# Attention on one Trainium2 core: the closing steps of a group loaded earlier and spread over the ticks

## The chip, the cores and the metric

The kernel runs on one core of a Trainium2 chip. A core has TensorE (PE, matrix products into PSUM), VectorE (DVE), ScalarE (ACT), GpSimd (POOL), and SyncE (SP), which in this kernel issues all DMAs. Each engine takes its instructions strictly in order. The metric is the device time of one execution in microseconds (us).

## The reference

A decoder trunk of two layers over 2048 tokens of width 1024. Layer 0 runs a gated recurrence (RG-LRU) and multi-head latent attention side by side, gates both with SiLU and projects them back; layer 1 is a Mamba-2 scan. What matters here is the attention of layer 0 and its gate:

```python
for blk in range(seqlen // Q_BLOCK):
    s = (jnp.einsum('bqhd,bkhd->bhqk', q_nope[:, q0:kend], k_nope[:, :kend])
         + jnp.einsum('bqhr,bkr->bhqk', q_rope[:, q0:kend], k_rope[:, :kend]))
    s = jnp.where(mask, s * scale, -jnp.inf)
    p = jax.nn.softmax(s, axis=-1)
    outs.append(jnp.einsum('bhqk,bkhd->bqhd', p, v[:, :kend]))
...
y = jnp.concatenate([y_rnn, y_mla], axis=-1) * jax.nn.silu(gate)
return jnp.einsum('bse,ed->bsd', y, w_out)
```

There are 8 heads, 64 value channels each. All matrix products are made in split precision: an operand is a high part and a low part, and three products (high-high, high-low, low-high) are summed, or two where one operand is exact enough.

## The kernel before

The program runs layer 0's projections and recurrence, then the attention (some 460 to 1005 us in the profile), the output projection of layer 0, the scan of layer 1 and its output projection. Between 1005 us and the end PE has few gaps.

**Groups.** Attention works in 32 groups. A group is a triple (pr, c, e): a pair of heads pr, a chunk c of 512 queries, and the head e of the pair. `GROUPS` (L35) lists them; a pair takes 8 groups, c from 3 down to 0, each for both heads (the last pair in another order). A group with chunk c looks at c+1 chunks of keys, so c=3 is the longest and c=0 the shortest. The texts number the groups 0 to 31 in this order: group 8 is the first of the second pair.

**Ticks.** One loop (L836 to 847) writes the program. For each group it goes through its score banks: `bank` (L736 to 751) makes three products of 128 queries with up to 512 keys (L740 to 742, on the diagonal also a mask, L744), and DVE takes the row maximum (L745). After each bank `tick()` advances a counter, and functions put off by `later(lag, fn)` are then written out. `expo` (ACT, L761), the sums (L769, L772) and the write of 1/sum to DRAM (L774) are put off in this way. L774 writes 128 x 4 numbers to a row of `d_li`, four bytes at a time. Between the banks of group n the loop writes the transposes (`trans`, L785) of the probabilities of the group before, each followed by a tick, then ACT's cast (L791), DVE's low part (`lo`, L129) and, five transposes later, the product with V (`pv`, L812).

**The split of q.** Group n+1 needs its q as high and low part in a slot of `ring`. `split_q(n + 1)` (L705 and one `lo`, both on POOL) stands after the second bank of group n, the load of q for group n+2 (`load_q`, L701) after the third. The first product of a group (L740) needs the first part, the third (L742) the second.

**The closing steps of a group.** `pv` adds up y for 512 queries in one PSUM bank. Two key blocks before its end SP loads 1/sum back from DRAM, spread over the 64 partitions of the head (`li`, L808), and the gate `g` (L809). The tiles `li`, `g` and `y` exist once, one half of the partitions for each head. When the last product is written, follow: one tick later ACT's copy of half of the bank to y (L818) and POOL's g*li (L819), after two ticks DVE's addition of the other half (L822), after three POOL's y*g (L826), after five the store of y (L829) to `d_y`. So POOL's queue holds L819 and L826 of one group right before a split of q for a later group, and SP's queue holds each store before later loads.

**After the last group** the loop from L865 drains what is left, and among it reads the first four tiles of `d_y` for the output projection (`out0_load`, L894) and splits two (L900). In the last groups POOL also splits six weight matrices for that projection (L114, L129).

Of the kernel before, what the change touches and what calls it, by code (L numbers as in the profile page):

```python
# [31 lines left out]
NV0 = 35  # L32


GROUPS = [(pr, c, e) for pr in range(4) for c in ((3, 1, 0, 2) if pr == 3 else (3, 2, 1, 0)) for e in range(2)]  # L35


EL, TL, LAG, SLACK = 3, 1, 5, 4
# [19 lines left out]
class K:  # L58
# [96 lines left out]
    def run(self):  # L155
        nc, tc, A = self.nc, self.tc, self.A
        with ExitStack() as ctx:
# [20 lines left out]
            D["x1T"] = dp.tile([NCH, P, KB, 2, 512], F32R, name="d_x1T")  # L178
            D["li"] = dp.tile([len(GROUPS), 512], F32, name="d_li")
            D["cs"] = dp.tile([NT, 32, P], F32, name="d_cs")  # L180
# [460 lines left out]
    def phase_qkv(self):  # L641
# [28 lines left out]
        self.qst = {}  # L670
        for n, (pr, c, e) in enumerate(GROUPS):
            if n < 8:
# [25 lines left out]
    def load_q(self, n):  # L698
        pr, c, e = GROUPS[n]
        self.qst[n] = self.stp.tile([P, 512], F32, tag="st", name="st")  # L700
        self.nc.sync.dma_start(out=self.qst[n], in_=self.D["q"][2 * pr + e, c])  # L701
# [6 lines left out]
    def phase_attn(self):  # L708
        nc, A, p, v = self.nc, self.A, self.at, self.nc.vector
        vv = self.W[:, 0:8, :].rearrange("p h (k n) -> p h k n", n=128)  # L710
        ring, D = self.ring, self.D
        N = len(GROUPS)

# [7 lines left out]
        prp = self.prp()  # L721
        prob, sums, accs = {}, {}, {}
        ready, flow = [], []

        def scores(n, i):

            pr, c, e = GROUPS[n]
            q = ring[:, 8 + n % 2, :]
# [48 lines left out]
        def trans():  # L777

            n, kb = ready.pop(0)
            pr, c, e = GROUPS[n]  # L780
            i0 = max(0, kb - 4 * c)
            ps = self.psum()
            for i in range(i0, 4):
                o = 512 * c * i + 64 * i * (i + 1) + kb * 128
                nc.tensor.transpose(ps[:, i * 128:i * 128 + 128], prob[n][:, o:o + 128], self.ident)  # L785
            self.cnt += 1
            k = self.cnt % 6
            hl = self.W[:, 8 + k // 2, k % 2 * 1024:k % 2 * 1024 + 1024] if k < 4 else ptx[:, k - 4]
            hl = hl.rearrange("p (s n) -> p s n", s=2)
            w = slice(128 * i0, 512)  # L790
            self.later(TL, lambda: nc.scalar.copy(hl[:, 0, w], ps[:, w]))  # L791
            self.later(TL + 1, lambda: self.lo(v, hl[:, 1, w], ps[:, w], hl[:, 0, w]))
            flow.append((n, kb, hl, w))
            if kb == 4 * c + 3:
                prob[n] = None
            if len(flow) > LAG:
                pv()
            self.tick()

        def pv():  # L800

            n, kb, hl, w = flow.pop(0)
            pr, c, e = GROUPS[n]
            nkb = 4 * c + 4
            if kb == 0:
                accs[n] = self.psum()
            if kb == nkb - 2:
                nc.sync.dma_start(out=li[half(e)], in_=D["li"][n].partition_broadcast(64))  # L808
                nc.sync.dma_start(out=g[half(e)], in_=D["sg"][pr, half(e), c * 512:c * 512 + 512])  # L809
            acc = accs[n]  # L810
            for s in range(2):
                nc.tensor.matmul(acc[:, w], vv[:, 2 * pr + e, kb], hl[:, s, w],  # L812
                                 start=(kb == 0 and s == 0), stop=(kb == nkb - 1 and s == 1))
            if kb == nkb - 1:
                r, o = half(e), half(1 - e)

                def copy():
                    nc.scalar.copy(y[r], acc[o])  # L818
                    nc.gpsimd.tensor_tensor(out=g[r], in0=g[r], in1=li[r], op=ALU.mult)  # L819

                def add():
                    v.tensor_tensor(out=y[r], in0=y[r], in1=acc[r], op=ALU.add)  # L822
                    accs.pop(n)

                def fin():
                    nc.gpsimd.tensor_tensor(out=y[r], in0=y[r], in1=g[r], op=ALU.mult)  # L826

                def store():
                    nc.sync.dma_start(out=D["y0"][4 * c:4 * c + 4, r, 4 + pr, :].rearrange("t p n -> p t n"),  # L829
                                      in_=y[r].rearrange("p (t n) -> p t n", n=P))  # L830
                self.later(1, copy)
                self.later(2, add)
                self.later(3, fin)
                self.later(5, store)

        for n in range(N):  # L836
            pr, c, e = GROUPS[n]
# [12 lines left out]
            k = n - (N - 9)  # L850
            if 0 <= k < 6:
                self.load_at(0, k, A["wo0"][k], 7, (nc.gpsimd, nc.gpsimd))
        k, old, ws = 0, True, []
# [11 lines left out]
        while ready or flow or any(d[1].__qualname__.endswith("expo") for d in self.defer):  # L865
            while todo and todo[0][0] <= k:
                todo.pop(0)[1]()
            if old and k > 3 and not any(x[0] < N - 1 for x in ready + flow):
                old = False
                self.later(2, lambda: last_w(0))  # L870
            k += 1
            if ready:
                trans()
            else:
                if flow:
                    pv()
                self.tick()
# [714 lines left out]
```

## Time and profile before

| | |
|---|---|
| median of three runs | 2729.05 us (2728.33 to 2729.82) |
| the profiled execution | 2731.9 us, of which the span of the program is 2729.8 |
| busy in the span | PE 2629.1 us (96%), DVE 1746.3, ACT 1532.1, POOL 940.2 |
| attention, from the first scores to the last product | 462.7 to 1005.4 us |
| granted clock of PE, mean | 0.985 |

A busy PE is not a PE at its peak, since matmuls overlap in the records. A row's idle time stands in brackets behind it, with what ended it. The page cuts the span into 40 slices of 68 us, and the row PEclk tells the granted clock in tenths of full speed (9 is 90% or more).

### The profile page before, as it was taken

How to read it: one execution, taken by the hardware profiler on the slowest of the kernel's cores; microseconds unless marked ns; L12 is line 12 of the kernel's file. 1: busy time of each engine (PE TensorE's matmuls, PEld its weight loads, DVE VectorE, ACT ScalarE, POOL GpSimd, SP SyncE). 2: the span in 40 equal slices, each digit the busy share in tenths (PEclk: the TensorE clock that was granted, in tenths of full speed). 3: DMA queues.
4: the chain of work that ended last, by engine and by line, in shares of the span. 5: the costliest groups of instructions: out<-in, count | busy, mean ns of one | idle time of the engine just before them, and what ended most of it. 6: DMA issues, size and time to landing. Idle time of an engine off the chain costs nothing.

```text
span 2729.8 us, 40041 instructions
## 1 busy us (share of the span) xinstructions
PE 2629.1 (96%) x14504; PEld 2168.2 (79%) x14504; DVE 1746.3 (64%) x3245; ACT 1532.1 (56%) x3178; POOL 940.2 (34%) x880
## 2 busy tenths in 40 slices
PE   8999999989898899999999999999999999899998
PEld 6888977868787777878888888888888888778886
DVE  7776236868686656775667766676677666745532
ACT  5664345757676652224667766776667667642100
POOL 5455320132324435452234323442244232433421
PEclk9999999989898999999999999999999999999999
DMA  4133337131424235666234333443234324456421
GB/s 146 53 95 103 109 112 262 35 68 41 69 44 81 65 105 193 214 237 192 79 125 157 124 110 106 146 142 110 99 122 143 110 102 141 158 175 216 164 106 39
DMA packets 173110, 334.22 MB, mean 122 GB/s; under 512 B 31985, under 2 KB 90225, under 8 KB 169457
## 3 DMA queue, kind: packets, MB, share of 16 engines
q1 hardware_dynamic: 172912, 331.66, 38.5%
q8 instruction: 115, 1.88, 0.3%
q14 instruction: 83, 0.67, 0.1%
HBM read 245.82 MB, written 85.79 MB: 121 GB/s over the span
## 4 chain that ended last, share of the span: by engine, by line
PE 68%; DVE 11%; DMA 7%; ACT 7%; issue 3%; POOL 2%; SPq 1%; POOLq 0%; ACTq 0%; DVEq 0%
PE ps L1148 8%; PE ps L1150 8%; PE ps L1149 8%; PE ps L137 5%; PE ps L139 5%; PE ps L138 5%; DMA g<-d_sg 3%; PE ps L1397 3%; PE ps L1398 3%; PE ps L1396 3%; PE ps L785 3%; PE ps L812 3%; PE ps L1251 2%; PE ps L910 1%; PE ps L742 1%
## 5 line engine op out<-in xcount | busy, mean ns | idle before, releaser
L1148 PE MATMUL ps<-ring,W 128*128 128x512 f32 x768 | 304.7, 397 | 0.0
L1150 PE MATMUL ps<-ring,W 128*128 128x512 f32 x768 | 300.2, 391 | 0.0
L1149 PE MATMUL ps<-ring,W 128*128 128x512 f32 x768 | 299.2, 390 | 0.0
L745 DVE TENSOR_REDUCE mx<-ps 128x1 f32<-128x512 f32 (+3 forms) x320 | 192.9, 607 | 114.3 <-PE ps L744 58.0
L1270 POOL TENSOR_TENSOR y<-y,xs 128x512 f32<-128x512 f32 x60 | 78.7, 1311 | 427.3 <-DVE y L1269 427.3
L761 ACT ACTIVATE pr<-ps,mx 128x512 f32<-128x512 f32 (+3 forms) x320 | 198.5, 629 | 14.9 <-DVE mx L749 10.0
L1148 PE MATMUL ps<-W,ring 128*128 128x512 f32 x512 | 201.3, 393 | 0.0
L1150 PE MATMUL ps<-W,ring 128*128 128x512 f32 x512 | 200.4, 391 | 0.0
L1149 PE MATMUL ps<-W,ring 128*128 128x512 f32 x512 | 199.9, 390 | 0.0
L785 PE MATMUL ps<-cst,pr 128*128 128x128 f32 x1088 | 181.3, 282 | 7.5 <-ACT pr L761 5.4
L1201 ACT ACTIVATE e<-e,tab 128x128 f32<-128x128 f32 x512 | 156.4, 390 | 42.6 <-DMA e<-d_cs 42.6
L1150 PEld LDWEIGHTS ps<-ring,W 128*128 128x128 f32 x768 | 144.1, 188 | 31.0
L1148 PEld LDWEIGHTS ps<-ring,W 128*128 128x128 f32 x768 | 144.4, 188 | 29.8 <-ACT yo L1302 0.9
L1149 PEld LDWEIGHTS ps<-ring,W 128*128 128x128 f32 x768 | 144.4, 188 | 28.9
L791 ACT CAST W<-ps 128x512 fp32r<-128x512 f32 (+2 forms) x213 | 110.8, 524 | 100.5 <-PE ps L785 98.6
L785 PEld LDWEIGHTS ps<-cst,pr 128*128 128x128 f32 x1088 | 133.9, 145 | 41.7 <-ACT pr L761 9.4
L129 DVE TENSOR_TENSOR W<-ps,W 128x512 fp32r<-128x512 f32 (+3 forms) x261 | 144.4, 559 | 30.6 <-ACT W L613 18.8
L740 PE MATMUL ps<-ring 128*128 128x512 f32 (+3 forms) x320 | 122.9, 384 | 37.6 <-POOL ring L705 34.4
L1116 ACT ACT_TABLE_LOAD x58 | 74.4, 1283 | 148.6 <-DVE xT L1114 79.2
L1381 ACT CAST ring<-ring 128x1024 fp32r<-128x1024 f32 x50 | 50.4, 1045 | 188.7 <-PE ps L1397 100.5
L129 POOL TENSOR_TENSOR ring<-ring 128x1024 fp32r<-128x1024 f32 (+1 forms) x41 | 84.1, 2051 | 190.4 <-ACT ring L1381 180.2
L129 POOL TENSOR_TENSOR W<-st,W 128x512 fp32r<-128x512 f32 (+2 forms) x70 | 111.4, 1597 | 103.7 <-ACT W L112 86.3
(347 smaller groups left out, 7552.3 us busy)
## 6 DMA issues: line engine op xcount, KB each, us to landing
ring<-d_x1T SPq DMA_DIRECT2D x128, 512.0 KB, 7.7
e<-d_cs SPq DMA_DIRECT2D x64, 512.0 KB, 4.5
ring<-d_y SPq DMA_DIRECT2D x25, 1024.0 KB, 7.8
st<-in_w_dram SPq DMA_DIRECT2D x40, 512.0 KB, 4.6
d_x1T<-xt SPq DMA_DIRECT2D x32, 512.0 KB, 3.1
d_y<-yo SPq DMA_DIRECT2D x64, 256.0 KB, 5.5
st<-in_wo_dram SPq DMA_DIRECT2D x24, 512.0 KB, 4.7
xs<-in_xT_dram SPq DMA_DIRECT2D x23, 512.0 KB, 4.3
```

Of the source, the lines that this page charges most:

```text
L129: eng.tensor_tensor(out=out, in0=src, in1=hi.bitcast(F32), op=ALU.subtract)
L137: self.nc.tensor.matmul(ps, ah, bh, start=(i == 0), stop=False)
L138: self.nc.tensor.matmul(ps, ah, bl, start=False, stop=False)
L139: self.nc.tensor.matmul(ps, al, bh, start=False, stop=(i == n - 1))
L740: nc.tensor.matmul(ps[:, 0:nw], qh, k[:, 0:nw], start=True, stop=False)
L745: v.tensor_reduce(out=m[:, kc:kc + 1], in_=ps[:, 0:nw], axis=AX.X, op=ALU.max, negate=True)
L761: nc.scalar.activation(out=prob[n][:, o:o + nw], in_=ps[:, 0:nw], func=AF.Exp, bias=nm, accum_out=acc)
L785: nc.tensor.transpose(ps[:, i * 128:i * 128 + 128], prob[n][:, o:o + 128], self.ident)
L1148: nc.tensor.matmul(ps, ah, bh, start=(k == 0), stop=False)
L1149: nc.tensor.matmul(ps, ah, bl, start=False, stop=False)
L1150: nc.tensor.matmul(ps, al, bh, start=False, stop=(k == KB - 1))
L1201: nc.scalar.activation(out=e[:, hd], in_=e[:, hd], func=AF.Relu, scale=-1.0, bias=cs[:, hd:hd + 1])
```

## The change

It does two things. In `pv` and in the steps behind it, the loads of `li` and `g` are written eight key blocks before a group's end (at the fourth block where the group is shorter) instead of two, and g*li, y*g and the store are cut apart: g*li moves from one tick after the last product to four, y*g from three to six, the store from five to ten; for c=0 to 8, 10 and 14. Before the loads of a group whatever is left of the last group of the same head is written out (`end[e]`). The copy (ACT) and the addition (DVE) stay. And the last pair takes its chunks in the order 3, 0, 1, 2 instead of 3, 1, 0, 2.

```diff
-GROUPS = [(pr, c, e) for pr in range(4) for c in ((3, 1, 0, 2) if pr == 3 else (3, 2, 1, 0)) for e in range(2)]
+GROUPS = [(pr, c, e) for pr in range(4) for c in ((3, 0, 1, 2) if pr == 3 else (3, 2, 1, 0)) for e in range(2)]
...
+        end = [lambda: None, lambda: None]
...
-            if kb == nkb - 2:
+            if kb == max(3, nkb - 8):
+
+                end[e]()
                 nc.sync.dma_start(out=li[half(e)], in_=D["li"][n].partition_broadcast(64))
                 nc.sync.dma_start(out=g[half(e)], in_=D["sg"][pr, half(e), c * 512:c * 512 + 512])
...
                 def copy():
                     nc.scalar.copy(y[r], acc[o])
+
+                def gate():
                     nc.gpsimd.tensor_tensor(out=g[r], in0=g[r], in1=li[r], op=ALU.mult)
...
                 self.later(1, copy)
                 self.later(2, add)
-                self.later(3, fin)
-                self.later(5, store)
+                left = [gate, fin, store]
+
+                def upto(k):
+                    while len(left) > k:
+                        left.pop(0)()
+                end[e] = lambda: upto(0)
+                for at, k in ((4, 2), (6, 1), (10, 0)) if c else ((8, 2), (10, 1), (14, 0)):
+                    self.later(at, lambda k=k: upto(k))
```

On SP, at the end of the first pair: the store of group 2 (d_y), the k loads for the next pair (ring<-d_k), the writes of 1/sum of groups 4 and 5 (d_li<-ls), the q loads of groups 7 and 8 (st<-d_q), the loads li and g of groups 3 and 4, and the store of group 3. Before:

```order
L829 DMA d_y_72<-y 64x4x128
L687 DMA ring<-d_k 64x1024
L774 DMA d_li<-ls_3759 128x4x1
L701 DMA st<-d_q 128x512
L808 DMA li<-d_li 64x512
L809 DMA g<-d_sg 64x512
L687 DMA ring<-d_k 64x1024
L829 DMA d_y_72<-y 64x4x128
L774 DMA d_li<-ls_3760 128x4x1
L701 DMA st<-d_q 128x512
L808 DMA li<-d_li 64x512
L809 DMA g<-d_sg 64x512
```

The same place now (L775, L811, L812 and L834 are the lines of the write of 1/sum, the two loads and the store):

```order
L834 DMA d_y_72<-y 64x4x128
L811 DMA li<-d_li 64x512
L812 DMA g<-d_sg 64x512
L775 DMA d_li<-ls_3759 128x4x1
L701 DMA st<-d_q 128x512
L687 DMA ring<-d_k 64x1024
L811 DMA li<-d_li 64x512
L812 DMA g<-d_sg 64x512
L775 DMA d_li<-ls_3760 128x4x1
L834 DMA d_y_72<-y 64x4x128
L701 DMA st<-d_q 128x512
L687 DMA ring<-d_k 64x1024
```

Each pair of loads li and g passed in front of a write of 1/sum and a q load; those of group 4 passed in front of the store of group 3 as well. The q load of group 8 stands behind that store in both.

On POOL, the same groups: g*li and y*g of groups 4 and 5, and the splits of q (L705 and L129) for groups 8 and 9. Before:

```order
L819 TENSOR_TENSOR g<-g,li 64x512
L826 TENSOR_TENSOR y<-y,g 64x512
L705 TENSOR_SCALAR ring<-st 128x512
L129 TENSOR_TENSOR ring<-st,ring 128x512
L705 TENSOR_SCALAR ring<-st 128x512
L129 TENSOR_TENSOR ring<-st,ring 128x512
L819 TENSOR_TENSOR g<-g,li 64x512
L826 TENSOR_TENSOR y<-y,g 64x512
```

And now:

```order
L824 TENSOR_TENSOR g<-g,li 64x512
L705 TENSOR_SCALAR ring<-st 128x512
L129 TENSOR_TENSOR ring<-st,ring 128x512
L831 TENSOR_TENSOR y<-y,g 64x512
L705 TENSOR_SCALAR ring<-st 128x512
L129 TENSOR_TENSOR ring<-st,ring 128x512
L824 TENSOR_TENSOR g<-g,li 64x512
L831 TENSOR_TENSOR y<-y,g 64x512
```

The split for group 8 passed in front of y*g of group 4; g*li of that group stays in front of it.

## Rows read from the trace of the kernel before

**Rows 1.** The page: its head, PE's busy time, the granted clock by slices
```profile
span 2729.8 us, 40041 instructions
...
PE 2629.1 (96%) x14504; PEld 2168.2 (79%) x14504; DVE 1746.3 (64%) x3245; ACT 1532.1 (56%) x3178; POOL 940.2 (34%) x880
...
PEclk9999999989898999999999999999999999999999
```

**Rows 2.** Table by stretch, the four pairs: span, busy by engine (instructions), PEclk, DMA share, GB/s
```profile
462.70:590.50 127.80, 114.08 (x675) 96.94 (x673) 97.00 (x216) 91.81 (x244) 24.68 (x23) 0.96 0.27 54
590.50:725.60 135.10, 122.53 (x705) 103.25 (x705) 100.30 (x224) 93.09 (x248) 35.51 (x32) 0.94 0.33 56
725.60:857.40 131.80, 120.50 (x705) 101.57 (x705) 100.25 (x224) 93.12 (x248) 35.57 (x33) 0.95 0.30 57
857.40:1005.40 148.00, 129.69 (x736) 108.39 (x737) 106.37 (x236) 99.34 (x258) 62.07 (x54) 0.92 0.35 84
```

**Rows 3.** Waits of PE, 440 to 1060 us: total, times, longest
```profile
PE ps L740 <- POOL ring L705: 34.4, 7, 8.9
...
PE ps L742 <- POOL ring L129: 5.1, 8, 0.9
PE ps L812 <- DVE W L129: 3.4, 1, 3.4
```

**Rows 4.** Waits of POOL, 440 to 1020 us
```profile
POOL g L819 <- DMA g<-d_sg: 266.1, 27, 17.3
```

**Rows 5.** Timeline of POOL: start, duration, instruction, idle before and what ended it
```profile
570.41 1.26 POOL L819 TENSOR_TENSOR g<-g,li 64x512 f32<-64x512 f32 x1 [12.69 <-DMA g<-d_sg]
...
587.26 1.25 POOL L819 TENSOR_TENSOR g<-g,li 64x512 f32<-64x512 f32 x1 [12.20 <-DMA g<-d_sg]
...
589.83 0.61 POOL L705 TENSOR_SCALAR ring<-st 128x512 fp32r<-128x512 f32 x1
...
598.74 1.28 POOL L819 TENSOR_TENSOR g<-g,li 64x512 f32<-64x512 f32 x1 [0.55 <-DMA g<-d_sg]
```

**Rows 6.** Timeline of SP, where the DMAs are issued
```profile
573.74 0.56 SPq L774 DMA_DIRECT2D d_li<-ls  x1
574.35 0.54 SPq L701 DMA_DIRECT2D st<-d_q  x1
...
575.45 0.59 SPq L809 DMA_DIRECT2D g<-d_sg  x1
...
592.37 0.59 SPq L809 DMA_DIRECT2D g<-d_sg  x1
```

**Rows 7.** Timeline of PE at full clock and after a wait
```profile
555.65 0.40 PE L742 MATMUL ps<-ring 128*128 128x512 f32 x1
555.89 0.60 PE L785 MATMUL ps<-cst,pr 128*128 128x128 f32 x4
556.25 0.70 PE L812 MATMUL ps<-W 128*128 128x512 f32 x2
556.78 0.34 PE L740 MATMUL ps<-ring 128*128 128x384 f32 x1
...
590.49 0.48 PE L740 MATMUL ps<-ring 128*128 128x128 f32 x1 [5.83 <-POOL ring L705]
...
592.98 0.63 PE L740 MATMUL ps<-ring 128*128 128x512 f32 x1
```

**Rows 8.** DMA issues, 462 to 1020 us: KB, median us to landing; then the q loads
```profile
g<-d_sg SPq DMA_DIRECT2D x32, 128.0 KB, 11.9
...
d_li<-ls SPq DMA_DIRECT2D x32, 2.0 KB, 9.4
...
DMA to landing us min/median/max: 2.0/3.5/11.6
```

**Rows 9.** Timeline of ACT, the first split of the output stage
```profile
994.88 1.04 ACT L900 CAST ring<-ring 128x1024 fp32r<-128x1024 f32 x1 [4.51 <-DMA ring<-d_y]
```

**Rows 10.** Waits of SP, 440 to 1060 us
```profile
SPq L829 <- POOL y L826: 213.0, 24, 15.6
```

## The prediction

> **What bounds the kernel now.** I read the page first. TensorE (PE) is busy 2629 of 2729.8 us [rows 1], so a change pays only where PE stands still or runs slowly. The change touches the attention stage, so next came a table by stretch over its four pairs of heads: 542.7 us, in which PE is busy 114 to 130 us of each 128 to 148, at a granted clock of 0.92 to 0.96 [rows 2]. In the page's slices the clock falls below nine tenths in this stage alone [rows 1], so something here makes it drop. The table of waits of PE names it: 34.4 us in 7 waits of the first score matmul of a group (L740) for POOL's split of q (L705), and 5.1 us in 8 waits of the third (L742) for the second half of that split [rows 3]. POOL is not overworked. It stands 266.1 us in front of L819, the product g*li, waiting for the load of g [rows 4], and the split of a later group stands behind L819 in POOL's queue.
>
> The timelines show the loop. With groups numbered in the order of GROUPS (8 to a pair; 3 is c=2 of the second head, 4 and 5 are c=1, 6 and 7 are c=0, 8 opens the next pair), L819 of group 3 starts at 570.41 and that of group 4 at 587.26, when the split of group 8 can follow at 589.83 [rows 5]. PE begins group 8 at 590.49 after 5.83 us of idling [rows 7]. L819 of group 4 was late because its load of g was issued only at 575.45 [rows 6], behind the store of group 3 (SP is in order, and the store waits for POOL's y*g), and because they came right behind a write of 1/sum in 4-byte elements (L774, 573.74) and a q load (574.35). From the issue of g to L819 it is 11.8 us (575.45 to 587.26), and 6.4 us (592.37 to 598.74) where the last L774 was long over [rows 5, 6]. The median landing is 11.9 for g and 9.4 for L774 [rows 8].
>
> **The change, part by part.** All counts stay: 32 each of L819, L826 and the store, 64 loads, at the same sizes. What changes is the place, and I measure places by a work clock: the PE instructions between two points, in issue order, each at the spacing that the rows show at full clock (a 512-column score matmul 0.23 to 0.24, four transposes 0.36, a pair of 512-column products 0.53, from start to start [rows 7], shorter ones by as much less as their own rows show). A pair of heads adds up to 113.7: 144 matmuls of full score banks 33.4, the diagonal banks 17.6, 272 transposes 24.5, 80 pairs of products 38.2. It took 135.1 and 131.8 in the second and third pair [rows 2].
>
> On this clock, from the start of a pair:
> - Group 3: load at 91.7 and gate at 93.4 before; 84.5 and 95.3 now. Group 4: 101.4 and 102.7 before; 97.5 and 104.7 now. So 1.7 and 1.3 us between issue and use become 10.8 and 7.2. For c=3 and c=2 it is 10.5 to 12 everywhere, for c=1 over 7, for the two c=0 groups 5 to 6.
> - The loads now stand before the L774 of the following group instead of behind it. So 6.4 us is the landing that I take, with 11.9 as the other end. With 6.4, the gate finds its data everywhere but at c=0, where no split is needed soon.
> - The split of group 7 is queued at 97.1 and needed at 101.7. With the load of g issued at about 85, gate and y*g are over by 97 and the split's halves by 98 to 99: no wait. With 11.9 the second half would be ready at about 101.6: still none.
> - The split of group 8 is queued at 105.3, needed at 109.0. With 6.4, group 4's gate is over at about 106; with 11.9 at 111.2.
>
> What goes, then, is 34.4 + 5.1 = 39.5 us of idling, and with it slow clock. The clock of the four pairs means 2 x (0.04 x 127.8 + 0.06 x 135.1 + 0.05 x 131.8 + 0.08 x 148.0) = 63 us at the lower level, 1.2 instead of 2.4 GHz [rows 2]; right after the wait of 590.49 a 512-column matmul shows 0.63 instead of 0.40 [rows 7]. If none of the idling lay in those 63 us, half of them, 32, would be lost; if all did, (63 - 39.5)/2 = 12. With half of it inside I take 21.5, and leave 3.5 of that with the wait at the end of the stage (below): 18. The gross gain is 57.5 us.
>
> What is late next is the q load of group 8 (L701). It was issued behind L774 of group 5 and the store of group 3, and still is: L774 at 98.0, the load at about 99.5. It was hidden behind the later gate before; now it ends last. The trace has a q load right behind an L774 landing after 11.6 us, the longest, against a median of 3.5 [rows 8]. One issued 1.5 us later I put at 10.5: landed at 110, first half of the split at 110.8 (0.61 [rows 5] and a start), so PE idles 1.8, and 0.7 more for the second half (5.1 in 8 waits [rows 3]). By the 3.5 it would idle nothing; by the 11.6, 3.5 in all. I take 2.5, plus 2 for the slow clock after it (the full waits had 18 / 7 = 2.6 each), at three turns of pairs: 13.5 back. A further 3 us in all goes to the 16 score banks of group 8, where DVE and ACT set the pace: they are busy about 100 and 93 us of a pair [rows 2], so 113.7 has little slack.
>
> On this the Trainium skill ("DMA: Bandwidth & Descriptors", Queues, rings and completion order) speaks against the change: descriptors of SP's one queue are consumed in ring order on each DMA engine, though completion is not strictly first in, first out. By it the q load can't pass the 512 small elements ahead of it and the turn keeps a wait, as in my sum; if loads overtook, the gross gain less 3 would stand. The 11.6 beside the 3.5 agrees with the rule.
>
> The other edits. The store waits behind a later y*g, and SP's queue behind it (li, g, q, k loads); at its tightest, the store of group 3 is due at 99.5, with y*g over at about 97: nothing. ACT's copy of the next group of the same head rewrites y and waits for that store: 11.6 us at least lie between them, more than L774's 9.4 ahead of the store. If that cover is gone, ACT and PE stop for the difference, up to 3 us at each turn. The new order of the last pair (c = 3, 0, 1, 2) has the same PE work. In its groups 26 to 29 POOL has four splits (0.61 and about 1.25), three gates with y*g (1.25 each) and four weight matrices (some 3.7 by the same sizes): 30 us beside 40 of PE. The order gets the c=0 tiles stored earlier, but the loads of the output stage still follow a store in SP's queue and come at the same work-clock place, so I leave the 3.4 us wait at 997 [rows 3], due to ACT standing 4.51 us before such a load [rows 9], and its 3.5 of clock. If they went too, 7 more would be gained.
>
> Sum: 57.5 - 13.5 - 3 = 41 us. After the stage PE is nearly gapless, so a shift there moves the end by as much. The profiled execution took 2731.9 (2729.8 of span and 2.1 around it): 2691. The median of the runs is 2.9 lower: 2688.
>
> **The rivals.**
> - *The q load isn't late.* It lands before PE gets to group 8, as PE itself comes a little later there. For it: the median of 3.5. Against: it stands behind L774. Gain 57.5 - 3 = 54: 2675; with the wait at the end gone as well, 2668.
> - *The waits move rather than go.* Loads of g still take 11.9. Group 8's split is then ready at 111.9 and 113.2, so PE idles 3.6 with 2.6 of clock after it, at three turns and once more in the last pair, where POOL has weights to split too: 4 x 6.2 = 25. Gain 57.5 - 25 - 3 = 30: 2699. For it: 27 waits of that kind now [rows 4]. Against: the loads pass in front of L774.
> - *The loop is the bound.* Store, li and g load, gate, y*g and store again took 16.85 us from gate to gate (570.41 to 587.26 [rows 5]), and 32 x 16.85 = 539, close to the 542.7 of the stage. In the new order the store of group n-1 still stands before the load of n in most groups. If the loop turns no faster, the stage takes 539: 2725, within the measurement. Against: with 6.4 instead of 11.8 a turn is 11.4.
> - *Slower: stores hold the q loads in SP's queue.* In the new order the q loads of groups 7 and 8 stand behind the stores of groups 2 and 3. Now SP stands 8.9 us on average in front of a store, 213.0 in 24 waits [rows 10]. If it still does, and the loads behind it land after 11.6, group 7's split (load at 86.8, needed at 101.7) is ready at 107.9 and PE idles 6.2; group 8's at 120.6, 11.6 late. With 0.7 and 2.6 for each that is 24.4 us a turn, against the 15.1 that the first three pairs lose each now ((57.5 - 12.2)/3, where 12.2 is the last pair's 8.9 [rows 3] + 0.7 + 2.6): 28 slower over three turns, less some 4 that the last pair still gains: 24, or 2753. It decides from a hold of about 4 us on. For it: that 213.0. Against: a store waits only where y*g is late, which with g in time it isn't.
>
> **How the numbers follow.** My forecast gets 0.5 (2678 to 2698 by itself), the q load in time 0.24, moved waits 0.16, the loop 0.05, held q loads 0.03, and something unseen that leaves the time the same 0.02. Below 0.2%, 5.5 us, a measurement can't tell a change from none. Faster is 0.5 + 0.24 + 0.16 and a bit of the loop's: 0.92; same 0.05; slower 0.03. The range runs from 2667, the lower end of the second case, to 2707, past the third.
>
> **What would show it.** The waits of L740 and L742 for POOL should fall from 39.5 to under 10 us, with those left at groups 8, 16 and 24 and POOL's split there released by the q load, no longer by what follows L819. POOL's wait for g should fall to well under 100 us and stand at the c=0 groups. From the issue of g to its landing it should be 6 to 7 us. The granted clock of the pairs should be 0.97 or more, the second and third pair 120 to 124 us long. I am wrong if g still lands after 11 to 12 us, if ACT waits at the copy of y for a store, if SP's q loads move with the stores, or if PE's waits turn into waits for ACT and DVE of the same size.

## The result, and the profile after

The changed kernel takes 2680.09 us (median of 4 runs, 2677.84 to 2684.56) against 2729.44 for the kernel before in the same series: a ratio of 0.9821, 95% interval 0.9804 to 0.9838. It is 49 us faster; 41 were forecast (2688 us). The profiled execution took 2678.24 us; by the two profiles the difference is 53.4 us (2729.8 to 2676.4 of span).

The head of the page of the changed kernel, PE's busy time and the granted clock by slices (before: [rows 1]):

```profile
span 2676.4 us, 40050 instructions
...
PE 2610.1 (98%) x14504; PEld 2153.2 (80%) x14504; DVE 1749.6 (65%) x3245; ACT 1531.1 (57%) x3178; POOL 944.2 (35%) x880
...
PEclk9999999999999999999999999999999999999999
```

PE executes the same 14504 matmuls in 19 us less busy time. The three slices below nine tenths are gone. The table by stretch, the four pairs (columns as in [rows 2]) and then the first tiles of the output stage:

```profile
461.60:576.90 115.30, 111.07 (x674) 94.52 (x672) 96.59 (x215) 90.71 (x243) 23.52 (x22) 1.00 0.31 60
576.90:700.50 123.60, 118.29 (x705) 99.85 (x705) 100.01 (x224) 92.55 (x247) 35.70 (x32) 0.99 0.34 59
700.50:824.70 124.20, 118.06 (x705) 99.61 (x705) 100.09 (x224) 93.24 (x250) 35.72 (x32) 0.98 0.30 62
824.70:957.40 132.70, 125.30 (x736) 104.32 (x737) 106.81 (x236) 99.31 (x258) 67.37 (x56) 0.98 0.47 92
...
957.30:1170.00 212.70, 209.81 (x1139) 172.22 (x1138) 152.21 (x247) 52.49 (x100) 102.68 (x91) 1.00 0.63 209
```

The same stretch of the output stage in the kernel before, which the rows ahead of the prediction don't hold:

```profile
1005.30:1222.90 217.60, 212.06 (x1140) 173.48 (x1139) 150.67 (x247) 52.54 (x100) 104.14 (x93) 0.99 0.61 204
```

Span less PE's busy time is PE's idling. Over the four pairs it fell from 55.9 to 23.1 us, and the busy time from 486.8 to 472.7: of the 46.9 us that the pairs lost, 32.8 are idling and 14.1 are busy time of the same matmuls, at a granted clock of 0.98 to 1.00 instead of 0.92 to 0.96. The output stage gave 4.9 more, the start of attention 1.1 (462.7 to 461.6), and the rest 0.5: 53.4 us of span.

The waits of PE, 440 to 1060 us, answer to [rows 3] (L740 and L742 are L741 and L743 now):

```profile
PE ps L741 <- POOL ring L705: 6.5, 3, 2.6
...
PE ps L743 <- POOL ring L129: 3.0, 4, 0.9
...
PE ps L815 <- DVE W L129: 1.4, 1, 1.4
```

From 39.5 us for the split of q, 9.5 are left. POOL's wait for g (440 to 1020 us, [rows 4] before, L824 now) and one row of SP's waits that was not there before:

```profile
POOL g L824 <- DMA g<-d_sg: 38.8, 15, 5.7
```

```profile
SPq L834 <- POOL y L831: 118.4, 25, 9.0
...
SPq L811 <- DMA d_li<-ls: 35.5, 10, 10.2
```

The row of [rows 10] is not all of SP's waiting for stores before the change. A second one, under the name of the instruction behind y*g in POOL's queue, belongs to it:

```profile
SPq L829 <- POOL ring L705: 106.9, 8, 14.4
```

So SP stood 319.9 us in front of stores, at all 32 of them; now it stands 126.0 (the 118.4 and three small rows). It now also stands 35.5 us in front of the early load of li, until the write of 1/sum that it reads has landed. That is the price of loading early in the short groups. At the turn to group 16 it stands 3.8 us there, until 687.09, and that group's q load (689.57), for which PE then waits, is behind it; how much of that wait comes from this was not separated.

What is left of the waits is the turn of a pair. POOL at the turn to group 8 (start, duration, instruction, idle before and what ended it):

```profile
565.37 1.29 POOL L824 TENSOR_TENSOR g<-g,li 64x512 f32<-64x512 f32 x1
576.25 0.62 POOL L705 TENSOR_SCALAR ring<-st 128x512 fp32r<-128x512 f32 x1 [9.60 <-DMA st<-d_q]
576.96 1.26 POOL L129 TENSOR_TENSOR ring<-st,ring 128x512 fp32r<-128x512 f32 x1
```

SP there, and PE behind it:

```profile
563.82 0.36 SPq L775 DMA_DIRECT2D d_li<-ls  x1
564.29 0.61 SPq L834 DMA_DIRECT2D d_y<-y  x1
564.95 0.59 SPq L701 DMA_DIRECT2D st<-d_q  x1
```

```profile
576.93 0.33 PE L741 MATMUL ps<-ring 128*128 128x128 f32 x1 [2.58 <-POOL ring L705]
...
578.27 0.33 PE L743 MATMUL ps<-ring 128*128 128x128 f32 x1 [0.91 <-POOL ring L129]
```

g*li, which held the split before [rows 5], is over at 566.7, and POOL idles 9.60 us for the q load, issued at 564.95 behind the write of 1/sum at 563.82. At groups 16 and 24 the split is released by the same load (at 699.81 and 824.01), with PE waiting 1.54 and 2.4 us. Last, the landings, 461 to 975 us (KB, median us), against [rows 8]:

```profile
st<-d_q SPq DMA_DIRECT2D x30, 256.0 KB, 11.1
...
li<-d_li SPq DMA_DIRECT2D x32, 128.0 KB, 3.4
g<-d_sg SPq DMA_DIRECT2D x32, 128.0 KB, 4.6
...
d_li<-ls SPq DMA_DIRECT2D x32, 2.0 KB, 12.0
```

g lands in 4.6 us instead of 11.9. These medians are of the landings that the trace tells, and they are few: g 8 of 32, q 9 of 30 and the write 8 of 32 here, 3, 4 and 3 before. So 11.1 beside the 3.5 of [rows 8], which holds stores of q as well, does not mean that the q loads have become slower. In the kernel with the order alone (below), whose first three pairs are those of the kernel before, the q loads of groups 8, 16 and 24 land after 11.1, 10.9 and 11.2 us (issued at 573.1, 707.6 and 840.5). So they were late without the change too, behind a wait for g that ended later still. In both kernels it is the transfer behind the write of 1/sum that is late.

### The profile page after: what moved, and what is told of

Same layout as the page of the kernel before. It is cut to its first block, busy times and chain, and to the rows that moved or that the text cites. A ratio compares the mean times of both kernels' runs of the same rounds, so it can differ in the third digit from the quotient of the medians.

```text
span 2676.4 us, 40050 instructions
## 1 busy us (share of the span) xinstructions
PE 2610.1 (98%) x14504; PEld 2153.2 (80%) x14504; DVE 1749.6 (65%) x3245; ACT 1531.1 (57%) x3178; POOL 944.2 (35%) x880
## 4 chain that ended last, share of the span: by engine, by line
PE 73%; DVE 10%; ACT 6%; DMA 5%; issue 3%; POOL 1%; SPq 0%; ACTq 0%; POOLq 0%; DVEq 0%
PE ps L1159 9%; PE ps L1161 9%; PE ps L1160 9%; PE ps L137 5%; PE ps L139 4%; PE ps L138 4%; PE ps L786 4%; PE ps L815 4%; PE ps L1409 3%; PE ps L1408 3%; PE ps L1407 3%; PE ps L1262 2%; PE ps L921 2%; PE ps L923 2%; PE ps L922 2%
## 5 line engine op out<-in xcount | busy, mean ns | idle before, releaser
L129 DVE TENSOR_TENSOR W<-ps,W 128x512 fp32r<-128x512 f32 (+3 forms) x261 | 145.0, 561 | 30.8 <-ACT W L613 18.8
L129 POOL TENSOR_TENSOR ring<-ring 128x1024 fp32r<-128x1024 f32 (+1 forms) x41 | 84.5, 2062 | 189.0 <-ACT ring L1392 160.1
L129 POOL TENSOR_TENSOR W<-st,W 128x512 fp32r<-128x512 f32 (+2 forms) x70 | 111.4, 1598 | 105.0 <-ACT W L112 90.2
L1125 DVE SCALAR_TENSOR_TENSOR xT<-ps,vec,xT 128x509 f32<-128x509 f32 (+2 forms) x192 | 143.2, 746 | 5.0
```

The source lines that it names most:

```text
L129: eng.tensor_tensor(out=out, in0=src, in1=hi.bitcast(F32), op=ALU.subtract)
L1125: v.scalar_tensor_tensor(out=dst, in0=src, scalar=w(k), in1=dst, op0=ALU.mult, op1=ALU.add)
```

## The experiments

The runs were made in three series, each on another chip, whose medians of the kernel before were 2730.41, 2737.38 and 2735.60 us. So kernels are compared by their ratio to the kernel before of their own series (intervals are 95%). The lengths of the pairs come from one profile each, as in the tables above, and they vary: the last pair is the same program in the changed kernel and in that with the q load on ACT's queue, and takes 132.6 and 139.8 us. A difference of some 7 us between two of these lengths shows nothing by itself.

| kernel | ratio (interval) | pairs 1 to 3, us | last pair, us |
|---|---|---|---|
| before | 1 | 394.7 | 147.9 |
| changed | 0.9821 (0.9804 to 0.9838) | 363.1 | 132.6 |
| early loads alone | 0.9883 (0.9866 to 0.9899) | 367.7 | 146.3 |
| spread and order | 0.9881 (0.9860 to 0.9903) | 375.3 | 135.6 |
| order alone | 1.0003 (0.9994 to 1.0013) | 392.6 | 147.0 |
| early loads and order | 0.9886 (0.9864 to 0.9907) | 367.3 | 148.9 |
| all, spread in the last pair alone | 0.9859 (0.9845 to 0.9874) | 372.9 | 140.5 |
| changed, q load earlier | 0.9789 (0.9770 to 0.9807) | 358.2 | 130.9 |
| changed, q load on ACT's queue | 0.9812 (0.9797 to 0.9828) | 366.4 | 139.8 |
| changed, 16-byte write | 0.9738 (0.9719 to 0.9756) | 351.9 | 127.9 |
| changed, waits added | 0.9913 (0.9897 to 0.9928) | 390.9 | 138.3 |
| before, 16-byte write and view | 0.9790 (0.9773 to 0.9806) | 357.1 | 135.0 |
| changed, 16-byte write and view | 0.9742 (0.9728 to 0.9757) | 351.1 | 128.0 |

**The early loads alone.**

```diff
-            if kb == nkb - 2:
+            if kb == max(3, nkb - 8):
```

> The kernel before with one edit: the loads of li and g stand eight key blocks before the end of a group (the fourth block where it is shorter); gate, y*g and store keep their old ticks, and the last pair its old order. If the place of the loads is what pays (the prediction's reason), POOL's wait for g falls from 266.1 us to under 90, the PE waits for POOL's split (34.4 + 5.1) to under 15, and the time to about 2688 (2682 to 2695). The rival, that the later ticks of gate and y*g keep POOL's queue open for the split, expects POOL to stand in front of y*g for the addition instead: PE waits above 20 us, time 2705 or more.

It gave 1.17%, or 32 us of 2729, where the whole change gives 49: less than the 34 to 47 that the first theory allowed, more than the 24 of the rival. POOL's wait for g fell as expected and PE's for the split nearly so, but a wait at the end of attention grew from 3.4 to 7.4 us. POOL, then PE, columns as before (line numbers of the kernel before):

```profile
POOL g L819 <- DMA g<-d_sg: 73.1, 16, 10.4
```

```profile
PE ps L740 <- POOL ring L705: 11.2, 4, 4.1
PE ps L812 <- DVE W L129: 8.8, 2, 7.4
...
PE ps L742 <- POOL ring L129: 3.9, 5, 0.9
```

So the loads alone give most of the gain of the first three pairs (27.0 of 31.6 us), and nearly nothing of the last (1.6 of 15.3).

**The spread, with the new order and the old place of the loads.** The diff is the one above, turned round, in the changed kernel.

> The changed kernel with the loads of li and g put back to two key blocks before the end; the later ticks of gate, y*g and store and the new order of the last pair stay. If the place of the loads pays, g still lands after 11 us or more and the split of groups 8, 16 and 24 still stands behind a waiting gate: PE waits for the split above 20 us, time 2705 to 2720. The rival, that the spread pays, expects PE waits under 12 us and 2680 to 2688.

It gave 1.19%, 32 us: also between the two. POOL still waits 201.5 us for g (landing 11.5), yet PE's waits fell to 18.3:

```profile
PE ps L741 <- POOL ring L705: 14.2, 4, 4.4
...
PE ps L743 <- POOL ring L129: 4.1, 5, 0.9
```

Each half of the change gives two thirds of the whole, and by group they relieve partly different waits. Before, PE waits for the first part of the split at groups 7, 15 and 23 (4.4, 3.6 and 0.6 us), at 8, 16 and 24 (5.8, 4.7 and 6.3) and at 30 (8.9). The early loads clear 7, 15 and 23; they leave 4.1, 3.6 and 1.6 us at 8, 16 and 24, and 1.9 at 30. The spread clears 8, 16, 24 and 30, and leaves 4.4, 4.0 and 4.2 us at 7, 15 and 23 (and 1.7 at group 28). The one lets g land sooner, the other lets POOL need it later.

**The order of the last pair alone.**

```diff
-GROUPS = [(pr, c, e) for pr in range(4) for c in ((3, 1, 0, 2) if pr == 3 else (3, 2, 1, 0)) for e in range(2)]
+GROUPS = [(pr, c, e) for pr in range(4) for c in ((3, 0, 1, 2) if pr == 3 else (3, 2, 1, 0)) for e in range(2)]
```

> The kernel before with the new order of the last pair alone (3, 0, 1, 2). The profile of the changed kernel gained 4.9 us in the output stage behind attention; if the order does that (the c=0 tiles are stored earlier), this kernel gains that, and part of the 8.9 us wait of group 30 with its clock: 2717 to 2725. If the 4.9 us come from the loads or the spread, and the 8.9 us wait only moves to another group: 2727 to 2731.

Nothing (1.0003). The 4.9 us of the output stage are not its work: that stretch takes 217.7 us here, but 212.7 with the early loads alone.

**The early loads with the new order, without the spread.** The two diffs above, in the kernel before.

> The kernel before with the early loads and the new order of the last pair, and gate, y*g and store at their old ticks. The early loads alone left 146.3 us in the last pair, where the changed kernel has 132.6. If the order is what was missing there (the c=0 tiles are stored before the output stage loads them, so ACT and PE don't wait at the end: 8.8 us), the last pair takes 133 to 137 and the time is 2684 to 2689. If it was the spread of gate, y*g and store, the last pair stays above 142 and the time at 2695 to 2702.

The order adds nothing to the early loads either (0.9886 against 0.9883); the last pair stays at 148.9. What is missing shows in ACT's waits at the end of attention, 900 to 980 us (L900 is the first split of the output stage):

```profile
ACT ring L900 <- DMA ring<-d_y: 8.9, 1, 8.9
```

With the early loads alone this wait is 8.5 us, before the change it was 4.51 [rows 9]; in the changed kernel it is not among ACT's waits. SP's timeline shows what differs. The early loads alone (L829 store, L862 loads of W, L894 loads of the output stage):

```profile
946.46 0.60 SPq L809 DMA_DIRECT2D g<-d_sg  x1
953.54 0.61 SPq L829 DMA_DIRECT2D d_y<-y  x1
954.19 1.30 SPq L862 DMA_DIRECT2D st<-in_wo_dram  x2
...
957.68 1.95 SPq L894 DMA_DIRECT2D ring<-d_y  x4
```

and the changed kernel (L834 store, L873 loads of W, L905 loads of the output stage):

```profile
930.22 0.52 SPq L775 DMA_DIRECT2D d_li<-ls  x1
930.78 1.21 SPq L873 DMA_DIRECT2D st<-in_wo_dram  x2
...
938.99 0.61 SPq L834 DMA_DIRECT2D d_y<-y  x1
939.70 2.30 SPq L905 DMA_DIRECT2D ring<-d_y  x4
```

With the store at its old tick SP stands from 947 to 953.5 in front of it, and 2 + 4 large loads go out in one bunch behind. With the later tick the loads of W pass ahead of the store, 9 us before those of the output stage.

**The spread in the last pair alone.** In the changed kernel:

```diff
-                for at, k in ((4, 2), (6, 1), (10, 0)) if c else ((8, 2), (10, 1), (14, 0)):
+                for at, k in ((1, 2), (3, 1), (5, 0)) if pr < 3 else ((4, 2), (6, 1), (10, 0)) if c else ((8, 2), (10, 1), (14, 0)):
```

> The changed kernel with the later ticks of gate, y*g and store in the last pair alone; the first three pairs have the old ticks, with the early loads. With the early loads alone, the first three pairs took 367.7 us (363.1 in the changed kernel, 394.7 before) and the last 146.3 (132.6 and 147.9). If the spread pays in the last pair alone, by letting SP pass the W loads and the loads of the output stage before the last stores, this kernel has 365 to 371 and 132 to 136, and a ratio of 0.982 to 0.985. If the last pair is short only because of what the first three leave, it stays above 142 and the ratio at 0.987 or more.

Neither: 0.9859, with 372.9 and 140.5 us. The wait for the output loads is gone (0.5 us on ACT), as the theory has it, but the spread is wanted in the first three pairs too. SP in this kernel at the turn to group 16:

```profile
693.78 0.62 SPq L834 DMA_DIRECT2D d_y<-y  x1
694.50 0.56 SPq L811 DMA_DIRECT2D li<-d_li  x1
...
696.39 0.50 SPq L701 DMA_DIRECT2D st<-d_q  x1
```

and in the changed kernel:

```profile
687.09 0.45 SPq L811 DMA_DIRECT2D li<-d_li  x1
...
688.90 0.61 SPq L834 DMA_DIRECT2D d_y<-y  x1
689.57 0.59 SPq L701 DMA_DIRECT2D st<-d_q  x1
```

At the old ticks the store stands ahead of the loads, SP waits in front of it for y*g until 693.78, and the loads and the q load go out 7 us later (2.3 of them since the pair began later). PE waits 6.4 us for group 16 instead of 1.5. That is what the spread is worth in the first three pairs: a store that is due later holds less behind it. The last pair's 140.5 us against 132.6 shows nothing, since the same program took 139.8 in another profile.

**The q load ahead of the write of 1/sum.** In the changed kernel:

```diff
-                if i == 2 and n + 2 < N:
+                if i == (0 if n + 2 in (8, 16, 24) else 2) and n + 2 < N:
```

> The changed kernel with the q loads of groups 8, 16 and 24 issued two score banks earlier (before the write of 1/sum of the group ahead, and before a store, instead of behind them); on PE, DVE, ACT and POOL nothing moves. If the q load lands late because it stands behind the 4-byte elements of that write, it lands now in 4 to 7 us instead of 11, the waits of groups 8, 16 and 24 (6.5 + 3.0 us) go under 1.5 in all, and with their slow clock the time comes to 2664 to 2672. If POOL's queue or the pace of DVE and ACT is next at that place, or the slow clock there has another cause, PE waits by another name and the time is 2676 to 2680.

The waits for POOL fell to 2.6 us (1.7 and 0.9), at one turn, and the pairs took 6.6 us less in all, of the 8 to 16 that were expected (two profiles can differ by as much). The median of the runs, 2674.89 us (2666.41 to 2678.27), lies between the two forecasts, and the interval of its ratio touches that of the changed kernel. At the turn POOL splits at 570.26, with no wait for the load that was issued at 561.23. So the load was late for its place; that all of the 9.5 us come back is not shown.

**The q load on ACT's queue, at its old place.**

```diff
-        self.nc.sync.dma_start(out=self.qst[n], in_=self.D["q"][2 * pr + e, c])
+        eng = self.nc.scalar if n in (8, 16, 24) else self.nc.sync
+        eng.dma_start(out=self.qst[n], in_=self.D["q"][2 * pr + e, c])
```

> The changed kernel with the q loads of groups 8, 16 and 24 issued by ACT, on its own DMA queue, at the same place in the program; nothing else moves. If the load is late because it stands behind the 4-byte elements in SP's queue, it lands in 4 to 6 us from its issue, the waits of the three groups (6.5 + 3.0 us) fall under 2 and the time is that of the run with the load issued earlier, 2668 to 2677. The rival, that the small elements keep the DMA engines themselves busy whatever the queue, expects 9 us or more, the same waits and 2677 to 2683.

No faster than the changed kernel (0.9812 against 0.9821). At group 8 the load is issued by ACT, 0.3 us behind the write of 1/sum on SP (564.40, L776 here), and used 12.8 us later; ACT and POOL:

```profile
564.71 0.35 ACTq L702 DMA_DIRECT2D st<-d_q  x1
```

```profile
577.51 0.62 POOL L706 TENSOR_SCALAR ring<-st 128x512 fp32r<-128x512 f32 x1 [10.22 <-DMA st<-d_q]
```

A queue of its own does not make the load behind that write land sooner here. (At the other two turns POOL's split was released by g or by PE, so they tell nothing.)

**The write of 1/sum in 128 elements of 16 bytes.** In the changed kernel:

```diff
-                    self.later(1, lambda: nc.sync.dma_start(out=D["li"][n].rearrange("(i p) -> p i", p=P), in_=ls[:, 4:8]))
+                    self.later(1, lambda: nc.sync.dma_start(out=D["li"][n].rearrange("(p i) -> p i", i=4), in_=ls[:, 4:8]))
```

> The changed kernel with 1/sum written in the order in which it lies in SBUF: 128 elements of 16 bytes instead of 512 of 4 (the rows of y then get the wrong 1/sum: this kernel leaves the right order out). If the number of elements sets how long that write and what stands behind it take, the write lands in 3 to 5 us instead of 12, the q load behind it in 4 to 7 instead of 11, the waits of groups 8, 16 and 24 go, and the time is 2666 to 2676. If the write's time is a fixed cost, or the q load is late for another reason, the q load stays at 9 or more and the time at 2677 to 2683.

By the ratio, 0.9738, it is 23 us better than the changed kernel (0.0083 of 2729), more than expected. The landings, 461 to 1010 us:

```profile
st<-d_q SPq DMA_DIRECT2D x30, 256.0 KB, 4.2
...
li<-d_li SPq DMA_DIRECT2D x32, 128.0 KB, 3.4
g<-d_sg SPq DMA_DIRECT2D x32, 128.0 KB, 3.5
...
d_li<-ls SPq DMA_DIRECT2D x32, 2.0 KB, 1.6
```

No wait of PE for POOL's split is left, and the granted clock is 1.00 in all four pairs.

**Longer waits at the turns.** In the changed kernel, the first half of the split of groups 8, 16 and 24 written eleven times:

```diff
-        nc.gpsimd.tensor_scalar(out=t[:, 0:512], in0=st, scalar1=1.0, scalar2=0.0, op0=ALU.mult, op1=ALU.add)
+        for _ in range(11 if n in (8, 16, 24) else 1):
+            nc.gpsimd.tensor_scalar(out=t[:, 0:512], in0=st, scalar1=1.0, scalar2=0.0, op0=ALU.mult, op1=ALU.add)
```

> The changed kernel with the first half of the split of groups 8, 16 and 24 written eleven times instead of once, so that PE waits 10 x 0.62 = 6.2 us longer at each of the three turns: 18.6 us more idling. This measures what a wait costs beyond itself. In the change itself attention lost 32.9 us of idling and 14.0 of PE's busy time (slow clock), 0.43 per us of idling. If the clock follows the idling so, the three pairs behind the turns show a granted clock of 0.94 to 0.96 and the time is 2680 + 18.6 x 1.43 = 2707 (2702 to 2711). If the idling costs only itself, 2697 to 2700; if PE makes part of it up (the banks of a turn are paced by DVE and ACT anyway), 2690 to 2696.

0.9913, which on 2729 is 25 us more than the changed kernel (0.0092), near the 27 expected. Yet the parts are not as expected. By the two profiles the waits grew by 24.1 us (30.6 at the three turns against 6.5, where 18.6 were meant), the idling of the pairs by 28.4 and PE's busy time by 5.0. These two profiles are of different series, and their pairs differ by 33.4 us where the ratios say 25, so the parts are rough. The first two of the four pairs:

```profile
462.80:586.90 124.10, 111.20 (x675) 94.75 (x674) 96.75 (x216) 91.32 (x244) 29.75 (x33) 0.97 0.33 59
586.90:720.20 133.30, 119.78 (x705) 101.28 (x705) 100.15 (x224) 93.06 (x248) 41.71 (x42) 0.95 0.30 54
```

The granted clock does follow the waits (0.95 to 0.97, from 0.98 to 1.00), but a us of idling cost some 0.18 us of busy time here, not the 0.43 of the change itself.

**The kernel before, with the 16-byte write and a view that puts li in order again.** The write is edited as in the run with 16-byte elements, and g*li so:

```diff
-                    nc.gpsimd.tensor_tensor(out=g[r], in0=g[r], in1=li[r], op=ALU.mult)
+                    gv = g[r].rearrange("d (i p) -> d i p", p=P)
+                    nc.gpsimd.tensor_tensor(out=gv, in0=gv, in1=li[r].rearrange("d (p i) -> d i p", i=4), op=ALU.mult)
```

> The kernel before with the same 16-byte write and view, and nothing of the change. If the slow write of 1/sum is the root of the waits and the change only walks around it, g lands 4 to 5 us after its issue instead of 11.9, POOL's wait for it falls from 266.1 to under 100 us, PE's waits for the split from 39.5 to under 10, and the ratio is 0.974 to 0.984. If the place of the loads (1.3 to 1.7 us before their use on the work clock) is a cause of its own, PE still waits over 15 us and the ratio is 0.986 or more.

0.9790: by itself at least as good as the whole change. PE's waits for the split are 6.3 us (39.5 before), g lands in 4.0 us, and POOL waits 146.3 us for it instead of 266.1, more than expected, though hardly where PE feels it. The slow write is the root of most of the waiting; the change walks around it.

**Both together.** The same two edits in the changed kernel.

> The changed kernel with 1/sum written in 128 elements of 16 bytes, and g*li on POOL reading li through a view that puts it back in order (4 elements apart), so that the result is the reference's. The run with the 16-byte write alone had a ratio of 0.9738 to the kernel before; if the view costs POOL nothing (g*li stays near 1.28 us), this one has 0.972 to 0.976. If the strided read slows g*li to 2.5 us or more, POOL gets to the splits later and the ratio is 0.976 to 0.981.

0.9742 (2666.31 us against 2735.60), the fastest that keeps the right order: 22 us under the changed kernel on the scale of 2729 (0.0079). The view lengthens g*li from 1.28 to 1.55 us (median of 32), which costs nothing that can be seen. What the change still adds to the cheap write is 0.0048, 13 us.

## Why the prediction came out as it did

The direction and the mechanism were right: PE stood still for a split that POOL had queued behind the wait for g, and most of the gain is that idling and the slow clock with it. Term by term, by the two profiles:

| term | forecast, us | measured, us |
|---|---|---|
| waits for the split, less those left at the turns | 39.5 - 7.5 = 32 | 39.5 - 9.5 = 30.0 |
| slow clock, less that behind the waits left | 18 - 6 = 12 | 14.1 of busy time |
| other idling in the pairs (pace of DVE and ACT, end of the stage) | -3 | 32.8 - 30.0 = +2.8 |
| start of attention, output stage, rest | 0 | 1.1 + 4.9 + 0.5 |
| sum | 41 | 53.4 of span |

The misses partly cancel: 2.0 us too much for the waits, 2.1 too little for the clock, 5.8 too little for the other idling, and 6.5 where nothing was put. The measured 2680 us is nearer to the rival "the q load isn't late" (2675) than to the forecast (2688), so the time alone doesn't tell the two apart; the 9.60 us that POOL stands before the q load of group 8 does, and it speaks for the forecast.

- **The turns of the pairs** went as worked out. PE idles 2.58 + 0.91 us at group 8 where 2.5 were put, at groups 8, 16 and 24 and nowhere else of that size, and the split there is released by the q load, 11.3 us from its issue (564.95 to 576.25; 10.5 was assumed). The granted clock is 0.98 to 1.00 (0.97 or more was asked), the second and third pair 123.6 and 124.2 us long (120 to 124). g lands in 4.6 us, better than the 6.4 assumed. POOL still waits for it outside the c=0 groups, which the prediction didn't expect (4.0 us at group 20, 5.1 at 28), but not where a split is late. The 3 us put for the pace of DVE and ACT did not come: PE's waits for ACT's exp are 10.5 us before and 9.6 after. And the median of 3.5 us on which the rival of the q load in time was given its 0.24 is one of four q loads and some stores; the q loads of the turns took 11.
- **The step that failed is the end of the stage.** The prediction left the wait of 3.4 us at 997, its clock, and the output stage as they were, since the loads there "still follow a store in SP's queue and come at the same work-clock place". That held for the four loads of the output stage: they go out 0.7 us behind a store and 17.6 us before the end of the stage (939.70 to 957.3), 16.9 before the change. What it missed is the two large loads of W ahead of them, which at the new ticks pass that store. The wait of 3.4 us is gone. What is left is one of 1.4 us nearer the end, which the early loads alone show too, beside their 7.4. The longest wait of this kind is 1.3 or 1.4 us in all the kernels with the new ticks in the last pair, and 3.4 to 7.8 in the four that have the old ticks and the slow write. The write has a share in it: with the old ticks and the 16-byte write the loads of W still go out only 2 us ahead of the four (935.7 and 937.6), yet ACT waits 2.2 us instead of 4.51, and PE's longest wait there is 1.4.
- **The output stage, put at nothing,** gave 4.9 us, and that with the early loads alone as well (212.7 us). POOL begins g*li of the last group 2.5 us behind the stage's start (959.8 to 957.3), before it was 7.1 (1012.4 to 1005.3), and the splits of the output stage stand behind it. In the three kernels where this is 6.5 us or more (before, spread and order, order alone) the stage takes 215.3 to 217.7 us, in the ten where it is 4.2 or less 212.6 to 214.3. That fits, but no run changed it alone, so the cause is not shown. The prediction had named 7 us for the case that the end is gained as well, but as 3.4 of waiting and 3.5 of clock inside attention; that 2.0 and 4.9 come near it is luck.
- **The credit was given to one half alone.** The working charged the later ticks with nothing and expected the whole gain from the place of the loads. The loads alone give 32 us, the ticks with the order 32, both 49. The rival "stores hold the q loads" priced the right mechanism, SP standing in front of a store; it had the sign wrong, because at the later tick the store holds less, not more. It also read only the first of two rows (213.0 of 319.9 us, 24 of 32 waits). With the early loads at the old ticks SP stands 229.4 us in front of stores, with the later ticks and the old loads 228.5, with both 126.0: each half takes some 90 off.
- **The reason for the late q load was half right.** Its place in time behind the write of 1/sum makes it late; being in the same queue is not needed. The rule of ring order in the Trainium skill ("DMA: Bandwidth & Descriptors", Queues, rings and completion order) was taken as the reason. Another place of the same page (Issuing engines are not separate DMA queues) says that loads issued by different engines run on the same 16 DMA engines, and that a second issuing engine saves issue time only. With that the run on ACT's queue agrees: 12.8 us at group 8. Nor is it the 512 elements themselves that keep the engines busy all that time. The packets of the changed kernel at that turn, from 564 to 566, from 567 to 575 and from 575 to 577 us:

```profile
DMA packets 678, 0.10 MB, mean 51 GB/s; under 512 B 530, under 2 KB 672, under 8 KB 677
DMA packets 134, 0.27 MB, mean 34 GB/s; under 512 B 14, under 2 KB 30, under 8 KB 134
DMA packets 780, 0.50 MB, mean 250 GB/s; under 512 B 575, under 2 KB 575, under 8 KB 780
```

The packets of the elements of the write issued at 563.82 are over by 566. Then, with the q load and a load of k issued, the engines move 34 GB/s for 8 us, and 250 right after. In the changed kernel with the 16-byte write they move 122 GB/s from 567 to 575, and a q load lands in 4.2 us. What the small elements leave behind that holds up other transfers, no run shows.
- **The clock.** The estimate of half the idling inside the slow stretches came within 2 us (12 against 14.1), but the added waits suggest that it is no constant: some 0.18 us of busy time per us of idling there, 0.43 in the change.

## What to carry to other kernels

When several transfers are late in turn, look for the one that lands ahead of each of them before moving any: here a write of 2 KB in 512 pieces delayed g, then q, and an edit of two statements that made it 128 pieces was worth at least as much as the whole rearrangement. In an in-order DMA queue a store that waits for its data holds every load behind it, so its place in the order is a cost of its own, beside when the data is ready. And price the end of a stage from the queue's order as well, not only from the work before it.

## What the hardware showed that was not expected

- The write of 1/sum in 512 elements of 4 bytes lands after 12.0 us (8.4 to 14.3), in 128 of 16 bytes after 1.9 (1.4 to 5.4): six times faster for a quarter of the elements and the same bytes. These are the medians in the changed kernel, the first of 8 landings told out of 32; in the kernel before they are 9.4 (of 3) and 2.8. The edit changes the number of the elements, their size and where neighbours lie in DRAM together; which of these counts was not tested. The Trainium skill ("DMA: Bandwidth & Descriptors", Rules for kernel authors) has the rule that a last dimension that isn't contiguous becomes one descriptor per element and should be rearranged; the two landings agree with it.
- A load on another queue, issued 0.3 us behind that write, was as late as one on the same queue: 12.8 us to its use, against 11.3.
- POOL reads an operand 4 elements apart at little cost: 1.55 us for 64x512 instead of 1.28.
